# More up tiles and empty steps beside two cross attentions, and inverse norms by VectorE with products against the identity, in a one-core encoder layer

## The chip, the cores and the metric

The kernel runs on one core of one Trainium2 chip. The metric is the device time of one execution in microseconds (us); less is better. Times of several executions are given as their median with the lowest and the highest.

## What is computed

One layer of a streaming encoder is applied to 1024 prompt frames and 32 sample frames of width 1024, in float32. The parts that the change touches are the norms, the cross attention into 256 memory tokens, and the start of the MLP:

```python
def rms_norm(x, g):
    y = x * lax.rsqrt(jnp.mean(x * x, axis=-1, keepdims=True) + EPS)
    return y * g

x = x + (sigmoid(ga) * a + sigmoid(gb) * bo) @ w_mix_out      # a: window attention, bo: short convolution
hc = rms_norm(x, g_cross)
cq = hc @ w_cq                                                # 4 heads x 64
p = softmax(cq @ mem_k * MEM_SCALE)
x = x + (p @ mem_v) @ w_co
hm = rms_norm(x, g_mlp)
x = x + square(relu(hm @ w_up)) @ w_down                      # hidden 4096
```

A final RMSNorm follows; keys, values, convolution state and memory keys and values are outputs too.

## The kernel before, in words

**Layout and arithmetic.** Activations are kept transposed: 128 features on the partitions, frames along the free dimension. The 1056 frames are cut into three chunks: c=0 and c=1 with 384 frames, c=2 with 288 (256 prompt, 32 sample). A float32 operand is split into a high part (rounded to float32r) and a low part (the rest); a product is the sum of three matmuls, hi*hi, hi*lo and lo*hi (`gemm`, L183 to L185). An output tile of 128 features and one chunk is 8 blocks of 3 matmuls, 24 in all. A helper, `split` (L125, L126), makes the two parts: ScalarE copies, VectorE subtracts.

**Weights.** `item(fn, key)` appends a work item and its weights to a plan. `run` walks the plan; `issue_w` loads a weight tile of 512 KB into a ring `wr` of two buffers, and splits it into rings `wh` and `wl` of three. Weights are issued in the order of the plan, at most three ahead. Of weights that come again (`kept`), the odd ones have their low part stored in HBM the first time and loaded (L156) after that.

**The planner.** The program text gives priorities; a planner then simulates the engines' times and writes each engine's order by that simulation: if the next instruction of an engine isn't ready in the simulation, a later one that is ready goes first. On the chip every engine runs its list in order. SyncE's list holds nearly all DMA issues.

**The stretch around the change.** `trunk(c)` is eight `do_conv_out` tiles and eight `do_mix` tiles of a chunk: output of the convolution merged with the gated attention, then the mixing projection and the residual. `pump(n)` splits what was loaded at the last pump and starts n more loads of the convolution's result (L786) into temporaries; all temporaries share one ring `ct` of six buffers (NCT). `cross_steps(c)` lists the steps of a chunk's cross attention: statistics of the first norm, the query projection `do_cq`, then a pipeline over heads (`Cross.scores`, `Cross.turn`, `Cross.values`; for c=2 the sample frames are a fifth unit, and it comes first), then the two halves of the output projection `do_co`, then the statistics of the MLP's norm. `beside(steps, fillers, late)` deals them out: after each filler tile one step, so that matmuls of the fillers stand between the dependent pieces of the steps. The order is: `trunk(0)` with pumps; `trunk(2)` beside the steps of c=0; `trunk(1)` beside those of c=2; then up tiles beside those of c=1. An up tile (`do_up(j, c)`) is a `gemm` of one of the first eight weight tiles of w_up with a chunk's normed activations, a relu and a square on GpSimd (L1244), and a store.

**After the cross attention of c=1.** `normed_split(1, f)` makes the normed and split activations of chunk 1, one of eight feature blocks at a time: a product on VectorE (L1212), a store, a copy on ScalarE (L1215), a difference on VectorE (L1216). They need R[1], the inverse norm of every frame on every partition, from `chunk_stats(1)`. Then come the up tiles of chunk 1, `combine(k)` (sums and differences of normed blocks for a Strassen-like scheme; for k of 2 and 3 half of it waits in `combine_rest` until the up tiles of chunk 1 are done), and `up_start`, which begins the 12 paired tiles of that scheme with weights from `up_fetch` (L1294, L1295) and `up_issue`.

**The inverse norm.** `square_acc` squares on ScalarE (L257) and adds on GpSimd (L259). `stats_col` sums over partitions by matmuls with a vector of ones (L214), giving one value per frame with frames on the partitions, 128 x 3; then v = mean + EPS on VectorE, a square root on ScalarE (L217), a reciprocal and one Newton step on VectorE (L218 to L221). `stats_row` spreads it: for each block of 128 frames the identity is multiplied by the column on ScalarE (L229), its low part is made on VectorE (L230), and two matmuls with a 128 x 128 matrix of ones (L231, L232) put every frame's value on all partitions in PSUM; `chunk_row` copies that to R[c] (L242). `stats_col` runs 13 times and `stats_row` 12 times: for the first norm of three chunks, the memory, both later norms of three chunks, and the final norm (where chunk 1 needs no row). For chunk 1 the last `stats_col` is followed only by six scalings (L1671, L1673) and the stores of the result.

## Time and profile before

| | |
|---|---|
| time, median of 3 runs (lowest to highest) | 1803.92 us (1800.46 to 1803.97) |
| profiled execution, its own time | 1799.48 us |
| profiled execution, from first to last instruction | 1797.6 us |
| TensorE matmul busy | 1757.5 us (98%) |
| VectorE / ScalarE / GpSimd busy | 65% / 44% / 33% |
| mean granted TensorE clock | 0.991 |

The profile is of one execution. PE is TensorE's matmuls, PEld its weight loads, DVE is VectorE, ACT is ScalarE, POOL is GpSimd, SP is SyncE, which issues DMAs. Matmuls overlap: each has its start, and its end is modelled, so PE is busy without a break when the next starts before the end of the last. A row of the timeline has the start in us from the first instruction, the duration, engine, source line, operation, the tile written and those read, shapes, count, and in brackets how long the engine was idle before and what it waited for. A row of a table by stretches has the stretch, its length, each engine's busy time (and instructions), the granted clock of TensorE as a share of full speed, and the load of the DMA engines (share, GB/s).

### The profile page before, as it was taken

What the parts mean: (1) busy time and instruction counts of PE and PEld (TensorE: products, weight loads), DVE (VectorE), ACT (ScalarE), POOL (GpSimd) and SP (SyncE); (2) the same over time, 40 slices, a digit from 0 to 9 for tenths busy, and PEclk for the clock granted to TensorE, in tenths of its full rate; (3) what the DMA queues carried; (4) which work ended last, traced back from release to release, by engine and by line L of the source; (5) the groups of instructions that cost most, each with busy time, mean ns of one, the idle gap of its engine ahead of it and who ended that gap; (6) DMA issues with size and microseconds to landing.
All of it is one profiled execution on the core that took longest, in us unless ns stands there. A gap on an engine that the chain in (4) does not pass through costs nothing.

```text
span 1797.6 us, 30252 instructions
## 1 busy us (share of the span) xinstructions
PE 1757.5 (98%) x11110; PEld 1737.5 (97%) x11110; DVE 1165.8 (65%) x2165; ACT 797.8 (44%) x1566; POOL 589.3 (33%) x681
## 2 busy tenths in 40 slices
PE   8999999999999999999999899899999999999997
PEld 8999999999999999999999899799999999999997
DVE  6776767868666746556575777667556676436773
ACT  8643535435344334335575656432222343324453
POOL 0013245653453534411233232375654300100111
PEclk9999999999999999999999999899999999999999
DMA  5232234344346888767766466653433487436573
GB/s 180 102 110 92 87 106 150 117 151 145 127 151 240 302 297 287 261 211 259 252 218 224 170 211 228 223 207 133 142 126 125 158 279 247 159 125 219 187 250 119
DMA packets 183859, 331.50 MB, mean 184 GB/s; under 512 B 18768, under 2 KB 139376, under 8 KB 183584
## 3 DMA queue, kind: packets, MB, share of 16 engines
q1 hardware_dynamic: 169936, 281.18, 46.3%
q0 software_dynamic: 13776, 48.41, 7.7%
q8 instruction: 87, 1.43, 0.3%
q14 instruction: 60, 0.49, 0.1%
HBM read 242.99 MB, written 86.52 MB: 183 GB/s over the span
## 4 chain that ended last, share of the span: by engine, by line
PE 85%; DMA 7%; DVE 3%; ACT 2%; issue 1%; POOL 1%; SPq 0%; DVEq 0%; ACTq 0%; POOLq 0%
PE acc L183 13%; PE acc L185 13%; PE acc L184 13%; PE acc L1606 6%; PE acc L1605 6%; PE acc L1607 6%; PE acc L851 5%; PE acc L852 5%; PE acc L853 5%; PE pa L184 2%; PE pa L183 2%; PE pa L185 2%; PE pt L572 2%; DMA wr<-in_w_conv_out 1%; DVE wl L126 1%
## 5 line engine op out<-in xcount | busy, mean ns | idle before, releaser
L126 DVE TENSOR_TENSOR wl<-wr,wh 128x1024 fp32r<-128x1024 f32 x225 | 297.2, 1321 | 177.2 <-ACT wh L125 175.2
L125 ACT CAST wh<-wr 128x1024 fp32r<-128x1024 f32 x225 | 236.2, 1050 | 384.0 <-PE acc L1606 104.1
L183 PE MATMUL acc<-X,wh 128*128 128x384 f32 (+1 forms) x864 | 282.1, 327 | 7.9 <-ACT wh L125 7.9
L184 PE MATMUL acc<-X,wh 128*128 128x384 f32 (+1 forms) x864 | 279.4, 323 | 0.0
L185 PE MATMUL acc<-X,wl 128*128 128x384 f32 (+1 forms) x864 | 278.7, 323 | 0.3 <-DVE wl L126 0.3
L185 PE MATMUL acc<-Y,wl 128*128 128x384 f32 (+1 forms) x624 | 201.9, 325 | 1.1 <-DMA wl<-wl_d 1.1
L184 PE MATMUL acc<-Y,wh 128*128 128x384 f32 (+1 forms) x624 | 202.5, 325 | 0.0
L183 PE MATMUL acc<-Y,wh 128*128 128x384 f32 (+1 forms) x624 | 199.4, 326 | 2.8 <-ACT Y L1215 1.8
L259 POOL TENSOR_TENSOR xacc<-xacc,ct 128x384 f32<-128x384 f32 (+1 forms) x62 | 72.3, 1168 | 361.8 <-ACT ct L257 360.0
L183 PEld LDWEIGHTS acc<-X,wh 128*128 128x128 f32 x864 | 163.2, 189 | 8.6 <-ACT wh L125 7.9
L184 PEld LDWEIGHTS acc<-X,wh 128*128 128x128 f32 x864 | 163.4, 189 | 0.6
L185 PEld LDWEIGHTS acc<-X,wl 128*128 128x128 f32 x864 | 163.1, 189 | 0.8 <-DVE wl L126 0.8
L183 PEld LDWEIGHTS acc<-Y,wh 128*128 128x128 f32 x624 | 117.5, 189 | 4.2 <-ACT Y L1215 2.2
L185 PEld LDWEIGHTS acc<-Y,wl 128*128 128x128 f32 x624 | 117.9, 189 | 1.7 <-DMA wl<-wl_d 1.7
L184 PEld LDWEIGHTS acc<-Y,wh 128*128 128x128 f32 x624 | 118.0, 189 | 0.0
L1606 PE MATMUL acc<-Y,wh 128*128 128x384 f32 (+1 forms) x352 | 113.2, 322 | 0.0
L1607 PE MATMUL acc<-Y,wl 128*128 128x384 f32 (+1 forms) x352 | 112.8, 321 | 0.0
L1605 PE MATMUL acc<-Y,wh 128*128 128x384 f32 (+1 forms) x352 | 112.5, 321 | 0.0
L125 ACT CAST PTh<-pt 128x512 fp32r<-128x512 f32 (+3 forms) x94 | 46.0, 516 | 112.3 <-PE pt L572 108.4
L707 POOL TENSOR_TENSOR ws<-ws 128x256 f32<-128x256 f32 x92 | 82.3, 895 | 5.2
L1244 POOL TENSOR_TENSOR ct<-ct 128x288 f32<-128x288 f32 (+1 forms) x48 | 45.7, 955 | 116.7 <-DVE ct L1240 52.6
L853 PE MATMUL acc<-Y,wl 128*128 128x384 f32 x248 | 83.3, 336 | 0.0
(360 smaller groups left out, 4755.7 us busy)
## 6 DMA issues: line engine op xcount, KB each, us to landing
wr<-in_w_in SPq DMA_DIRECT2D x53, 512.0 KB, 3.7
wr<-in_w_up SPq DMA_DIRECT2D x48, 512.0 KB, 3.8
wr<-in_w_down SPq DMA_DIRECT2D x32, 512.0 KB, 3.9
wr<-wsum_d SPq DMA_DIRECT2D x32, 512.0 KB, 3.6
wl<-wl_d SPq DMA_DIRECT2D x28, 512.0 KB, 4.5
wr<-in_w_conv_out SPq DMA_DIRECT2D x24, 512.0 KB, 4.8
wr<-in_w_mix SPq DMA_DIRECT2D x24, 512.0 KB, 4.7
ct<-b_d SPq DMA_DIRECT2D x48, 192.0 KB, 3.9
```

Of the source, the lines that this page charges most:

```text
L125: act.copy(hi, src)
L126: dve.tensor_sub(lo, src, hi.bitcast(F32))
L183: pe.matmul(out, wh[:, a], hi, start=(k == 0), stop=False)
L184: pe.matmul(out, wh[:, a], lo, start=False, stop=False)
L185: pe.matmul(out, wl[:, a], hi, start=False, stop=(k == len(acts) - 1))
L707: pin(pool_e.tensor_tensor(t[:, to], t[:, x], t[:, y], op=ALU.add))
L851: pe.matmul(acc, wh[:, a], hi, start=(start and k == 0), stop=False, skip_group_check=True)
L852: pe.matmul(acc, wh[:, a], lo, start=False, stop=False, skip_group_check=True)
L853: pe.matmul(acc, wl[:, a], hi, start=False, stop=(k == 3), skip_group_check=True)
L1605: pe.matmul(a, wh[:, s], hi, start=(start and k == 0), stop=False, skip_group_check=True)
L1606: pe.matmul(a, wh[:, s], lo, start=False, stop=False, skip_group_check=True)
L1607: pe.matmul(a, wl[:, s], hi, start=False, stop=(stop and k == len(acts) - 1), skip_group_check=True)
```

## The change

1. **Fillers.** All eight up tiles of chunk 2 stand beside the cross attention of c=1, where five did; the other three stood after the up tiles of chunk 1.
2. **Steps.** For c=2 and c=1 the list of steps no longer begins with an empty step, so the first statistics come after the first filler and not after the second. For c=2 an empty step is put after the scores of the first unit and another before `do_co`. The steps of c=1 end after the twelfth of 16 fillers.
3. **normed_split(1)** is dealt out three after the 14th, three after the 15th and two after the 16th filler.
4. **After it** `combine(k)` follows up tile 0, 2, 4, 6 of chunk 1 (before: 1, 3, 5, 7); `up_fetch` and `up_issue` follow tiles 5 and 7 of chunk 1 (before: 6 and 7 of chunk 2); both `combine_rest` come after all up tiles of chunk 1.
5. **Pumps** in `trunk(0)`: three loads after each of the first five tiles and none after the sixth (before: two after each of the eight).
6. **Inverse norm.** The start value comes from an integer shift and a multiply-add on the bit pattern, followed by three Newton steps, all on VectorE; the square root, the reciprocal and the early call that loads its table go. The column is split into high and low parts of 128 x 3, and each is used, broadcast along the free dimension, as the stationary operand against the identity: six matmuls of 128 columns take the place of two over the whole row, and the six products with the identity on ScalarE and VectorE go.

```diff
-        v, s, y, t = (misc.tile([P, nb], F32, tag=x, bufs=2, name=nm(x)) for x in ("st_v", "st_s", "st_y", "st_t"))
+        v, y, t = (misc.tile([P, nb], F32, tag=x, bufs=2, name=nm(x)) for x in ("st_v", "st_y", "st_t"))
         dve.tensor_scalar(v, pq, 1.0 / D, EPS, op0=ALU.mult, op1=ALU.add)
-        act.activation(s, v, AF.Sqrt)
-        dve.reciprocal(y, s)
-        dve.tensor_mul(t, v, y)
-        dve.scalar_tensor_tensor(t, t, -0.5, y, op0=ALU.mult, op1=ALU.mult)
-        dve.scalar_tensor_tensor(rcol, t, 1.5, y, op0=ALU.add, op1=ALU.mult)
+        dve.tensor_single_scalar(t.bitcast(I32), v.bitcast(I32), 1, op=ALU.arith_shift_right)
+        dve.tensor_scalar(y.bitcast(I32), t.bitcast(I32), -1, 0x5F3759DF, op0=ALU.mult, op1=ALU.add)
+        for to in (y, y, rcol):
+            dve.tensor_mul(t, v, y)
+            dve.scalar_tensor_tensor(t, t, -0.5, y, op0=ALU.mult, op1=ALU.mult)
+            dve.scalar_tensor_tensor(to, t, 1.5, y, op0=ALU.add, op1=ALU.mult)
...
         pr = ps.tile([P, n], F32, tag="pt", bufs=2, name=nm("pr"))
-        dh, dl = tmp(n, F32R), tmp(n, F32R)
+        rh, rl = (misc.tile([P, len(blocks)], F32R, tag=x, bufs=2, name=nm(x)) for x in ("st_h", "st_l"))
+        dve.tensor_copy(rh, rcol)
+        dve.tensor_sub(rl, rcol, rh.bitcast(F32))
         for j, b in enumerate(blocks):
-            s, r, eye = slice(j * P, b + P), rcol[:, j : j + 1], ident[:, j * P - b :]
-            act.mul(dh[:, s], eye, r)
-            dve.scalar_tensor_tensor(dl[:, s], eye, r, dh[:, s].bitcast(F32), op0=ALU.mult, op1=ALU.subtract)
-        pe.matmul(pr, ones_r, dh, start=True, stop=False)
-        pe.matmul(pr, ones_r, dl, start=False, stop=True)
+            s, eye = slice(j * P, b + P), ident_r[:, j * P - b :]
+            for r in (rh, rl):
+                pe.matmul(pr[:, s], r[:, j : j + 1].to_broadcast([P, P]), eye, start=(r is rh), stop=(r is rl))
...
-        act.copy(ones_r, ones.to_broadcast([P, P]))
-        warm = misc.tile([P, 1], F32, name="warm")
-        act.activation(warm, ones, AF.Sqrt)
         make_identity(nc, ident)
+        act.copy(ident_r, ident)
...
-        steps = [("call", [mem_load] if c == 0 else [])]
+        steps = [("call", [mem_load])] if c == 0 else []
...
-            if c == 0 and i < nu:
+            if c == 0 and i < nu or c == 2 and i < 1:
                 steps.append(("call", []))
...
+        if c == 2:
+            steps.append(("call", []))
         steps.append(("items", [(do_co(c, 0), ("w_co", 0))]))
...
-    left = beside([], trunk(0), [(i, lambda: pump(2)) for i in range(NF)])
-    item(lambda: pump(0))
+    left = beside([], trunk(0), [(i, lambda i=i: pump(3 if i < 5 else 0)) for i in range(6)])
...
-    left = beside(left + cross_steps(1), up0(0) + up0(2)[:5])
+    left = beside(left + cross_steps(1), up0(0) + up0(2), normed(1, (13, 13, 13, 14, 14, 14, 15, 15)))
     assert not left
-    for f in range(NF):
-        item(lambda f=f: normed_split(1, f))
     for j in range(NF):
         item(*do_up(j, 1))
-        if j in (1, 3, 5, 7):
+        if j in (0, 2, 4, 6):
             item(lambda k=j // 2: combine(k))
-    for j in range(5, NF):
-        item(*do_up(j, 2))
-        if j < 7:
-            item(lambda k=j - 3: combine_rest(k))
-        if j == 6:
+        if j == 5:
             item(lambda: [up_fetch(0), up_fetch(1), up_issue(0, 1)])
         if j == 7:
             item(lambda: [up_issue(0, 2), up_issue(1, 1)])
+    item(lambda: [combine_rest(k) for k in (2, 3)])
```

More of the change, by code (lines that the diff above doesn't have):

```diff
@@ L12 @@
 F32R = mybir.dt.float32r
+I32 = mybir.dt.int32
 AF = mybir.ActivationFunctionType
@@ L68, in hybrid_step @@
     ones = misc.tile([P, 1], F32, name="ones")
-    ones_r = misc.tile([P, P], F32R, name="ones_r")
+    ident_r = misc.tile([P, P], F32R, name="ident_r")
     nsink = misc.tile([P, 20], F32, name="nsink")
```

## The prediction, made before the changed kernel was run

> **What bounds the kernel now.** I read the page first, then what TensorE waits for, then a table of stretches, then the timeline where the table shows a hole. The first lines of the page:
>
> ```profile
> span 1797.6 us, 30252 instructions
> ...
> PE 1757.5 (98%) x11110; PEld 1737.5 (97%) x11110; DVE 1165.8 (65%) x2165; ACT 797.8 (44%) x1566; POOL 589.3 (33%) x681
> ```
>
> TensorE is the bound, with 40.1 us idle in all. A reordering can only win back idle time and the slow clock that follows it; more matmul time is paid in full. The longest of TensorE's waits:
>
> ```profile
> PE acc L183 <- ACT wh L125: 9.8, 4, 7.9
> ```
>
> 7.9 us of it is the start, which waits for a weight and isn't touched. The rest lies in few places, which the stretches show:
>
> ```profile
> 820.00:860.00 40.00, 37.01 (x190) 35.71 (x189) 26.13 (x42) 19.70 (x36) 6.56 (x6) 0.91 0.72 241
> 1000.00:1040.00 40.00, 34.75 (x207) 33.25 (x206) 32.08 (x70) 26.17 (x68) 11.84 (x12) 0.91 0.44 149
> 1118.00:1160.00 42.00, 33.66 (x175) 30.85 (x176) 25.84 (x45) 19.11 (x32) 14.90 (x13) 0.88 0.63 217
> 1160.00:1187.00 27.00, 26.94 (x168) 26.70 (x167) 18.12 (x25) 12.40 (x19) 17.60 (x15) 1.00 0.95 332
> 1240.00:1280.00 40.00, 40.00 (x252) 40.00 (x252) 25.40 (x33) 9.77 (x11) 24.14 (x19) 1.00 0.40 135
> 1136.36:1146.60 10.24, 6.91 (x20) 6.39 (x21) 5.92 (x14) 3.51 (x8) 0.00 (x0) 0.50 0.44 149
> 1020.31:1023.71 3.40, 3.40 (x17) 3.38 (x17) 2.33 (x6) 1.73 (x5) 0.00 (x0) 0.50 0.01 3
> ```
>
> 1240 to 1280 is how it runs undisturbed. The three stretches on top are the seams of this change: the pumps' end, the end of the cross attention of c=2, and the passage to the up tiles of chunk 1. There the granted clock falls to half for 3.4 us or a multiple after a wait, so a hole costs its idle time and more.
>
> **The hole of chunk 1** (fillers, normed_split and combine, one edit). After the fifth up tile of chunk 2:
>
> ```profile
> 1133.67 0.83 PE L214 MATMUL pq<-ones,xacc 128*128 128x1 f32 x6 [0.80 <-POOL xacc L259]
> 1137.87 0.69 PE L231 MATMUL pr<-ct,ones_r 128*128 128x384 f32 x1 [3.37 <-ACT ct L229]
> 1140.78 1.01 PE L183 MATMUL acc<-Y,wh 128*128 128x384 f32 x2 [1.82 <-ACT Y L1215]
> ```
>
> TensorE sums, waits for the column, spreads it, waits for the first normed block. In 1118 to 1160 it is idle 42.00 - 33.66 = 8.3 us; of the 10.24 us at half clock it works 6.91, which loses 3.5. The hole costs 11.8 us. In the new order four up tiles of chunk 2 stand between the statistics and the first up tile of chunk 1. Their step:
>
> ```profile
> 1132.32 0.29 PE L183 MATMUL acc<-Y,wh 128*128 128x288 f32 x1
> 1132.44 0.29 PE L184 MATMUL acc<-Y,wh 128*128 128x288 f32 x1
> ```
>
> They start 0.12 us apart (0.125 with what rounding hides), so 24 matmuls take 3.0 us and four tiles 12. The chain from the column's sum (1133.67) to the first normed block (1140.78) took 7.1 us, so it is covered with 4.9 to spare, in which further blocks get ready. Two things remain: the 0.80 for GpSimd's squares, since one tile stands before the sum as now, and about 1.5 us of shorter waits for weights and for `do_co`'s operand. I take -9.5; ends 0 (the planner consumes the tiles earlier) and -11.8.
>
> What moves past what: the weights of three up tiles (one load of 512 KB each, a second for the odd ones) go ahead of chunk 1's on SP; the eight normed_split (on DVE twice, ACT once, SP once each) share VectorE and the six `ct` buffers with up tiles that they had nearly to themselves; the four combine (four loads each on SP, three differences on DVE, one on POOL, four splits) come one tile earlier. Nothing of this is on TensorE's path while fillers last.
>
> **The passage to `up_start`.** The three tiles of chunk 2 stood between the up tiles of chunk 1 and the first paired tiles, and covered their weights. That cover goes. SP's rows:
>
> ```profile
> 1175.96 0.33 SPq L145 DMA_DIRECT2D wr<-in_w_up  x1
> 1179.75 0.33 SPq L1294 DMA_DIRECT2D wr<-in_w_up  x1
> ```
>
> The first half of pair 0 is loaded 3.8 us behind the last up weight, less than a tile's time (4.2): the pair's weights simply continue the sequence and come as the next weight would. The DMA engines were full in 1160 to 1187 (0.95, 332 GB/s) and TensorE didn't wait; three weights fewer fall into that stretch now. `combine_rest` has the 17 us of `up_start` as its cover (48 matmuls of 384 columns at 0.175, priced below, and three tiles of 3.0). Bounds 0 and +10 (a hole like the one removed); I take +1, near the row that shows no wait.
>
> **Cross attention of c=2.**
>
> ```profile
> 1019.14 0.38 PE L1156 MATMUL o<-PTh,mv 128*128 128x256 f32 x1 [2.90 <-DVE tO L1159]
> ...
> 1025.42 0.66 PE L1183 MATMUL acc<-Y,wh 128*128 128x288 f32 x3 [1.34 <-ACT Y L1165]
> ```
>
> In 1000 to 1040 TensorE is idle 5.25 us, and the clock (0.91 of 40 us) takes 3.6 more: 8.9. Values of the last heads and the output projection run there with no filler between. The first unit begins a filler earlier and has one more behind it, and one mixing tile of 24 x 0.175 = 4.2 us now stands before `do_co`; the 1.34, the second slow stretch and the small waits should go. The 2.90 has another root:
>
> ```profile
> 1017.09 0.61 ACT L262 ACTIVATE Y<-Ga,prm 128x384 fp32r<-128x384 f32 x1 [1.33 <-DVE Ga L1045]
> ```
>
> ScalarE stood behind a residual whose load came late, and the copy that frees the buffer `o` stood behind that. The empty step moves this only by chance. I take -5; ends 0 and -8.9.
>
> **Pumps.**
>
> ```profile
> 823.20 1.01 POOL L1031 TENSOR_TENSOR ct<-ct,ct 128x384 f32<-128x384 f32 x1 [4.87 <-DMA ct<-m_d]
> 830.36 1.02 POOL L1031 TENSOR_TENSOR ct<-ct,ct 128x384 f32<-128x384 f32 x1 [6.14 <-DMA ct<-m_d]
> ...
> 833.75 0.45 PE L184 MATMUL acc<-M,wh 128*128 128x384 f32 x1 [0.69 <-DVE M L126]
> ```
>
> The merge of one tile follows the last by 7.2 us, against 4.2 of matmuls, because its second operand waits for one of six `ct` buffers, four of which the pumps hold; by the eighth tile the lag reaches the mixing tiles. 820 to 860 costs 3.0 idle and 3.6 by the clock, 6.6. Without pumps the last three tiles have the buffers to themselves; but with three loads instead of two in the first five the lag builds up earlier. Ends -6.6 and +6.6 (the same hole, earlier); I take -2, as the lag has three tiles to shrink.
>
> **The spreading of the norm.** From the chain of waits, where each piece is the time to the next, and from the groups:
>
> ```profile
> 1082.53 0.18 PE acc L183
> ...
> 1089.24 0.66 PE pt L1137 x6
> ```
> ```profile
> L231 PE MATMUL pr<-ct,ones_r x12: 279/333/688, 35.8 to 1738.7; 128*128 128x384 f32 x7, 128*128 128x288 f32 x4, 128*128 128x256 f32 x1
> ```
>
> A matmul of 384 columns steps by 0.175, one of 128 columns by 0.11: six take 0.66, two took 0.35. So +0.31 seven times, +0.40 four times (two of 288 at 0.125 went), and +0.2 for the memory (four for two): +4.0 us, in full, since these stand between fillers. Ends 0 (they fall into waits) and +8 (half clock). The Trainium skill, "TensorE: Matmul & The Clock Gate", section "Back-to-back issue gap", gives about 81 ns for a matmul of 128 columns with its weight load; by that figure the estimate would be +2.0 and the sum 2 us lower; the row here, of transposes of the same width, says 0.11.
>
> **The column on VectorE.** Six more dependent steps; on ScalarE these go, with the square root itself:
>
> ```profile
> 1134.40 1.28 ACT L217 ACT_TABLE_LOAD   x1
> ...
> 1136.83 0.98 ACT L229 ACTIVATE ct<-ident,rc 128x128 fp32r<-128x128 f32 x3 [0.88 <-DVE rc L221]
> ```
>
> ScalarE is 44% busy and such chains otherwise run beside fillers: 0, between -2.3 where a chain is waited for (1.28 + 0.98) and what the first rival below costs. At the end of the program nothing hides the steps:
>
> ```profile
> 1788.47 0.16 DVE L216 TENSOR_SCALAR st_v<-pq 128x3 f32<-128x3 f32 x1 [2.93 <-PE pq L214]
> ...
> 1789.50 0.16 DVE L221 SCALAR_TENSOR_TENSOR rc<-st_t,st_y 128x3 f32<-128x3 f32 x1
> 1789.69 2.07 DVE L1671 TENSOR_SCALAR y<-acc,rc 128x512 f32<-128x512 f32 x3
> ```
>
> From the sum to the first scaling 1.2 us; twelve steps at the pitch of 0.2 take 2.4: +1.2 (ends +0.7 and +2).
>
> **The sum.** -9.5 + 1 - 5 - 2 + 4.0 + 1.2 = -10.3 us. The profiled execution took 1799.48 (span 1797.6 and 1.9 around it), which gives 1789.2. The median of the runs shown is 4.4 above that execution, so the forecast for the median is 1803.92 - 10.3 = 1793.6, taken as 1793.5. What a measurement of this kernel can tell from no change is about 0.2%, 3.6 us.
>
> **The rivals.**
>
> *Late R blocks the accumulators (slower).* The evictions of `do_cq` need R and hold two of three accumulators until it comes:
>
> ```profile
> 974.85 0.82 DVE L1089 SCALAR_TENSOR_TENSOR ct<-acc,R 128x288 f32<-128x288 f32 x2 [1.14 <-ACT R L242]
> ```
> ```profile
> 1066.53 1.54 DVE L126 TENSOR_TENSOR wl<-wr,wh 128x1024 fp32r<-128x1024 f32 x1
> ```
>
> In the second row a weight's low part slid in between two links of the chain. If that happens before each of the six new links, a chain is 6 x (1.2 + 0.2) = 8.5 us longer, less the 2.3 that goes; with one free accumulator, some 2 us of slack (half a tile of 24 x 0.175), TensorE waits 4 us at each of three query projections, and 1.7 by the clock: +17, which gives 1810.6. It decides from 14 us in all, some 3 us of wait at each. For it: the slid-in row; against: the planner knows the links. 0.13.
>
> *The hole moves to `up_start`.* If the pair's first weight finds both `wr` buffers held, TensorE waits for load, cast and difference at the end of chunk 1: +9 on top, 1802.6. The full DMA speaks for it, the rows of SP against it. 0.17.
>
> *All seams close.* -11.8 - 8.9 - 6.6 + 5.2 = -22: 1781.8. Nothing excludes it. 0.12.
>
> *The clock isn't tied to these waits.* Only idle time would come back: 6 of the 8.3 at chunk 1, 2.6 of the 5.25 at c=2, 1 of the 3.0 at the pumps, less 5.2 and 1: -3.4, 1800.5. The Trainium skill's same page, section "What's actually happening", has the clock fall only after an idle window of about 3.4 us; by that rule these waits, none of them longer than 3.37 in the rows above, would not lower it. The trace speaks against it: half clock at 1020.31 follows 2.90 idle and is seen nowhere in 1240 to 1280. 0.06.
>
> **Numbers.** The forecast with errors of its terms, 1788 to 1799, has 0.47; 0.05 is left for what I don't see, on both sides. Range 1782 to 1804: it leaves out the late R and about half of the full closing. Faster by over 0.2% (under 1800.3): 0.47 + 0.12 + 0.03 of the clock rival + 0.06 of the moved hole + rest = 0.72; the same: 0.09; slower: 0.19.
>
> **What would show it.** Chunk 1: no wait of L231 or its successor for the column, L183 not waiting for L1215, full clock from the statistics to the up tiles; if wrong, a wait of L183 or L851 for `wh` or `wl` at `up_start`. c=2: no wait before L1183, the 2.90 perhaps still there. Pumps: L1031 at an even pace and no wait for M; if wrong, waits for L1030 while the first five tiles run. Spreading: 46 matmuls more, 0.11 apart. End: 2.4 us from L214 to L1671. The prediction is wrong if the planner's new order opens a seam that isn't there now, since every engine's list is written anew.

## The result, and the profile after

The changed kernel takes **1814.08 us** (median of 4 runs, 1811.75 to 1815.9) against 1802.19 for the kernel before (1800.43 to 1803.97). The ratio is 1.0065, with a 95% interval of 1.0046 to 1.0084. It is slower by 11.9 us where 10.3 less were forecast. The profiled execution took 1812.96 us, 13.5 more than that of before.

The page's first lines, after:

```profile
span 1811.2 us, 30363 instructions
...
PE 1761.4 (97%) x11156; PEld 1739.9 (96%) x11156; DVE 1185.2 (65%) x2245; ACT 776.2 (43%) x1509; POOL 586.9 (32%) x681
```

TensorE has the 46 matmuls more, and 3.9 us more work (1757.5 before). Its idle time grew from 40.1 to 49.8 us. So 9.7 of the 13.6 us by which the span grew are waits. In the table of what TensorE waits for, these two are the largest behind the start:

```profile
PE acc L184 <- DVE ct L1030: 8.0, 2, 6.9
PE acc L186 <- DMA wl<-wl_d: 4.3, 1, 4.3
```

Line numbers are shifted by one here: L184 to L186 are the three matmuls that were L183 to L185. In the first, 6.9 of 8.0 us are one wait; the second is a single one. The table by stretches (length, busy time of PE, PEld, DVE, ACT, POOL, then clock, DMA share and GB/s) says where the kernel loses, as the prediction's table did for before:

```profile
820.00:860.00 40.00, 32.01 (x173) 31.24 (x173) 24.93 (x42) 18.07 (x36) 6.19 (x6) 0.91 0.69 219
1000.00:1060.00 60.00, 53.96 (x316) 51.04 (x314) 46.89 (x92) 36.04 (x90) 19.73 (x18) 0.94 0.49 170
1118.00:1160.00 42.00, 39.46 (x270) 37.34 (x268) 25.52 (x49) 20.05 (x31) 16.36 (x16) 1.00 0.70 250
1160.00:1187.00 27.00, 21.63 (x105) 20.06 (x106) 15.09 (x25) 9.30 (x15) 8.09 (x8) 0.87 0.84 272
```

Idle time and half clock can't simply be added here, since half clock costs nothing while TensorE waits. What counts is the time that it works at half clock:

```profile
833.75:840.58 6.83, 3.42 (x11) 3.45 (x12) 4.90 (x9) 3.37 (x8) 1.00 (x1) 0.50 0.90 305
1175.09:1181.91 6.82, 4.52 (x14) 4.52 (x15) 3.06 (x5) 1.87 (x3) 3.16 (x3) 0.50 1.03 384
```

TensorE works 3.42 and 4.52 us of these two stretches, and half of that is lost. So the pumps cost 8.0 idle and 1.7 by the clock, 9.7, against 6.6 before. The second row is the cross attention of c=2 (60 us here, since it lies later): 6.0 idle and 3.1 by the clock, 9.1, against 8.9. In the last two rows the hole has moved. 1118 to 1160 lost 11.8 before and now 2.5 at full clock; 1160 to 1187 lost nothing before and now 5.4 idle and 2.3 by the clock, 7.6. The timeline of TensorE shows the new hole, and that of the DMA queue on SP what stands ahead of the load that it waits for:

```profile
1177.39 0.69 PE L186 MATMUL acc<-Y,wl 128*128 128x384 f32 x1 [4.27 <-DMA wl<-wl_d]
```
```profile
1160.53 1.42 SPq L1213 DMA_DIRECT2D xn_d<-ct  x2
1166.05 0.32 SPq L1263 DMA_DIRECT2D lt<-xn_d  x1
1166.47 0.38 SPq L1213 DMA_DIRECT2D xn_d<-ct  x1
...
1170.28 0.91 SPq L1263 DMA_DIRECT2D lt<-xn_d  x2
1171.24 0.48 SPq L157 DMA_DIRECT2D wl<-wl_d  x1
```

Between 1161.95 and 1166.05 SP issues nothing. Its own table of waits over 1150 to 1180 says why:

```profile
SPq L1263 <- DMA xn_d<-ct: 6.5, 2, 4.0
```

`combine` loads normed blocks that `normed_split` has just stored, so its load waits 4.0 us for the store to land. The low part that TensorE waits for is issued behind it, at 1171.24, and lands 6.1 us later. The stall is not what delays it, though. VectorE takes finished up tiles of chunk 1 out of the accumulators (L1242) at these times:

```profile
1170.58 0.56 DVE L1242 TENSOR_SCALAR ct<-acc 128x384 f32<-128x384 f32 x1 [3.27 <-PE acc L186]
...
1171.52 0.55 DVE L1242 TENSOR_SCALAR ct<-acc 128x384 f32<-128x384 f32 x1
...
1172.63 0.55 DVE L1242 TENSOR_SCALAR ct<-acc 128x384 f32<-128x384 f32 x1
```

Three tiles run interleaved, as the normed blocks arrive, and end together. The wait stands at the fourth tile (the texts put on record with the experiments call it the second). Its low part goes into the ring `wl` of three buffers, of which the first comes free when the first tile ends, at about 1170.5. The load leaves 0.7 us after that, so SP's list costs at most 0.7. In the kernel before, three tiles end together too; there SP stands idle from 1152.6 on and waits for TensorE to give the buffer back (its table of waits over 1152 to 1156):

```profile
SPq L156 <- PE acc L185: 3.3, 1, 3.3
```

That load leaves at 1155.69 and lands 3.5 us later, where the changed kernel's takes 6.1. The DMA engines are 97% busy while the latter is under way, and 73% during the former. That the loads of `combine`, bunched behind the stall, are what slows it is likely, but no run shows it.

### The profile page after: what moved, and what is told of

Same layout as the page of the kernel before. It is cut to its first block, busy times and chain, and to the rows that moved or that the text cites. A ratio compares the mean times of both kernels' runs of the same rounds, so it can differ in the third digit from the quotient of the medians.

```text
span 1811.2 us, 30363 instructions
## 1 busy us (share of the span) xinstructions
PE 1761.4 (97%) x11156; PEld 1739.9 (96%) x11156; DVE 1185.2 (65%) x2245; ACT 776.2 (43%) x1509; POOL 586.9 (32%) x681
## 5 line engine op out<-in xcount | busy, mean ns | idle before, releaser
L184 PE MATMUL acc<-X,wh 128*128 128x384 f32 (+1 forms) x864 | 282.4, 327 | 8.2 <-ACT wh L126 8.2
L185 PE MATMUL acc<-X,wh 128*128 128x384 f32 (+1 forms) x864 | 279.6, 324 | 0.0
L186 PE MATMUL acc<-X,wl 128*128 128x384 f32 (+1 forms) x864 | 278.9, 323 | 0.3 <-DVE wl L127 0.3
L184 PE MATMUL acc<-Y,wh 128*128 128x384 f32 (+1 forms) x624 | 202.1, 328 | 9.1 <-DVE ct L1030 8.0
L186 PE MATMUL acc<-Y,wl 128*128 128x384 f32 (+1 forms) x624 | 203.0, 326 | 4.3 <-DMA wl<-wl_d 4.3
L185 PE MATMUL acc<-Y,wh 128*128 128x384 f32 (+1 forms) x624 | 203.4, 327 | 0.9 <-DVE Y L1216 0.9
L184 PEld LDWEIGHTS acc<-X,wh 128*128 128x128 f32 x864 | 163.2, 189 | 8.9 <-ACT wh L126 8.2
L185 PEld LDWEIGHTS acc<-X,wh 128*128 128x128 f32 x864 | 163.6, 189 | 0.6
L186 PEld LDWEIGHTS acc<-X,wl 128*128 128x128 f32 x864 | 163.3, 189 | 0.8 <-DVE wl L127 0.8
L184 PEld LDWEIGHTS acc<-Y,wh 128*128 128x128 f32 x624 | 118.1, 190 | 11.7 <-issue 7.2
L186 PEld LDWEIGHTS acc<-Y,wl 128*128 128x128 f32 x624 | 118.4, 190 | 4.6 <-DMA wl<-wl_d 4.6
L185 PEld LDWEIGHTS acc<-Y,wh 128*128 128x128 f32 x624 | 118.6, 190 | 1.7 <-DVE Y L1216 1.7
L852 PE MATMUL acc<-Y,wh 128*128 128x384 f32 x248 | 83.8, 338 | 0.0
L851 PE MATMUL acc<-Y,wh 128*128 128x384 f32 x248 | 83.7, 338 | 0.0
```

Source lines behind the costliest of these rows:

```text
L184: pe.matmul(out, wh[:, a], hi, start=(k == 0), stop=False)
L185: pe.matmul(out, wh[:, a], lo, start=False, stop=False)
L186: pe.matmul(out, wl[:, a], hi, start=False, stop=(k == len(acts) - 1))
L851: pe.matmul(acc, wh[:, a], hi, start=(start and k == 0), stop=False, skip_group_check=True)
L852: pe.matmul(acc, wh[:, a], lo, start=False, stop=False, skip_group_check=True)
```

## The experiments

Each single edit was put on the kernel before, then parts were undone in the changed kernel, then the parts that gained were put together. Ratios are against the kernel before on the same chip, whose median was between 1802 and 1807 in these comparisons; 0.01% is 0.18 us.

| kernel | median, us | against before | interval |
|---|---|---|---|
| the whole change | 1814.08 | +0.65% | +0.46 to +0.84 |
| pumps alone | 1808.18 | +0.26% | +0.12 to +0.41 |
| norm alone | 1813.38 | +0.36% | +0.23 to +0.50 |
| steps of c=2 alone | 1812.30 | +0.30% | +0.14 to +0.45 |
| fillers alone | 1803.21 | -0.14% | -0.26 to -0.01 |
| pumps, ring of their own | 1799.75 | -0.33% | -0.48 to -0.17 |
| spreading alone | 1813.08 | +0.35% | +0.21 to +0.48 |
| column alone | 1814.11 | +0.39% | +0.23 to +0.54 |
| column, one Newton step | 1802.67 | -0.16% | -0.28 to -0.04 |
| empty steps of c=2 alone | 1801.68 | -0.27% | -0.43 to -0.12 |
| first step of c=2 dropped, alone | 1818.99 | +0.58% | +0.39 to +0.78 |
| fillers, low parts not kept | 1809.01 | +0.19% | +0.07 to +0.31 |

The four single edits sum to +0.78%, 14 us, which lies within the interval of the whole; the sum itself is uncertain by some 0.3%. The two halves of the norm do not add: +0.35% and +0.39% alone, +0.36% together. Two theories were put against each other: that every edit pays at its own place, or that the rewritten lists open holes anywhere.

### A second profile of the kernel before

No edit; it says how far two profiles of one program differ.

> The kernel before once more, for a second profile: the one shown took 1799.48 us and was the fastest of its runs. If its small losses were luck, waits that no edit touches are longer here: the wait for the gate at 684 (L962), 0 there and 1 to 2 us in the traces of the single edits, and the wait for the low weight part at the second up tile of chunk 1, 1.05 there and 2.6 to 5.2 in the others. If those waits come from the edits, both are again under 1.1.

It took 1808.0 us against 1799.48 for the profile of the prediction. TensorE's timeline, at three places:

```profile
684.88 0.41 PE L851 MATMUL acc<-X,wh 128*128 128x384 f32 x1 [1.50 <-DVE Ga L962]
...
1131.24 0.50 PE L1183 MATMUL acc<-Y,wh 128*128 128x384 f32 x1 [2.58 <-DVE ct L1240]
...
1164.58 0.44 PE L185 MATMUL acc<-Y,wl 128*128 128x384 f32 x1 [1.25 <-DMA wl<-wl_d]
```

The first wait was not there at all, the second was 0.35, the third 1.05. So the profile shown was a lucky one, and a difference of 1 to 3 us at one place between two single profiles says nothing by itself. It also says that the wait for `wl_d` stood in the kernel before already: what causes it is not new.

### The pumps

```diff
-    left = beside([], trunk(0), [(i, lambda: pump(2)) for i in range(NF)])
-    item(lambda: pump(0))
+    left = beside([], trunk(0), [(i, lambda i=i: pump(3 if i < 5 else 0)) for i in range(6)])
```

> The kernel before with the new pumps alone (three loads after each of the first five convolution tiles, none after the sixth). Theory 1 (every part pays at its own place): the wait for L1030 that the changed kernel has at 829.9 (6.89 us and half clock behind it) comes from the three loads in the ring of six temporaries, so it stands here too; 820 to 880 loses about 5 more than before, and the time is 1807. Theory 2 (the lists are written anew and the hole is an accident of the new order): no wait of 6.9 for L1030 here, and the time is within 3 us of 1802. The prediction's own term was -2: 1800.

+0.26%, and the wait stands where it stood in the whole change, with the same releaser:

```profile
825.68 0.42 PE L183 MATMUL acc<-Y,wh 128*128 128x384 f32 x1 [2.09 <-DVE ct L1030]
...
837.70 0.66 PE L183 MATMUL acc<-Y,wh 128*128 128x384 f32 x1 [7.61 <-DVE ct L1030]
```

So it is the edit's own. Whether the cause is the ring of six or SP's order, the next kernel decides: same pumps, and (once the cross attention's pool is open) a ring of three more buffers for what they load.

```diff
-wanted.extend((bcp[c], k, bc_d[c][:, k], CH[c][1], lambda c=c: yslot(c)) for k in range(NF))
+wanted.extend((bcp[c], k, bc_d[c][:, k], lambda c=c: cr.tile([P, CH[c][1]], F32, tag="pm", bufs=3, name=nm("pm")) if cr else tmp(CH[c][1]), lambda c=c: yslot(c)) for k in range(NF))
```

> The new pumps alone, but the loads of the pumps go into a ring of three buffers of their own instead of the shared ring of six. Theory 1 (three loads in the ring of six take the buffers that the evictions and the merge's operand need): the wait for L1030 at 829 (7.6 us with the new pumps) is under 1.5, the hole with its half clock is gone, and the time is 0.4% below that of the new pumps with the shared ring, at or below before. Theory 2 (the hole comes from SP's order: the merge's operand is loaded behind two weights and three pump loads, 6 us to landing): the wait stays at 4 or more, and the time is within 0.1% of the new pumps alone.

From +0.26% to -0.33%: the ring. The stretch 820 to 880 of the two kernels, shared ring first:

```profile
820.00:880.00 60.00, 50.30 (x282) 49.72 (x281) 35.38 (x55) 28.75 (x51) 12.12 (x11) 0.94 0.74 237
```
```profile
820.00:880.00 60.00, 57.06 (x343) 55.94 (x342) 42.37 (x62) 31.84 (x53) 14.22 (x12) 1.00 0.81 269
```

9.7 us idle become 2.9, and the clock stays up. The merges on GpSimd follow each other at 4.0 and 4.3 us, and the last two at 6.0 and 5.5, where the prediction quoted 7.2 for before:

```profile
814.04 1.10 POOL L1031 TENSOR_TENSOR ct<-ct,ct 128x384 f32<-128x384 f32 x1 [2.52 <-DMA wr<-in_w_conv_out]
818.06 1.94 POOL L1031 TENSOR_TENSOR ct<-ct,ct 128x384 f32<-128x384 f32 x1 [2.92 <-DVE ct L1030]
822.40 1.00 POOL L1031 TENSOR_TENSOR ct<-ct,ct 128x384 f32<-128x384 f32 x1 [2.40 <-DMA ct<-m_d]
828.38 1.87 POOL L1031 TENSOR_TENSOR ct<-ct,ct 128x384 f32<-128x384 f32 x1 [4.98 <-DVE ct L1030]
833.84 1.25 POOL L1031 TENSOR_TENSOR ct<-ct,ct 128x384 f32<-128x384 f32 x1 [3.59 <-ACT Y L781]
```

What the three buffers would do for the old pumps was not run, so the gain against before isn't split between the pumps and the buffers.

The same edit of the ring in the changed kernel, all else as it is:

> The changed kernel with one thing changed: the loads of the pumps have a ring of three of their own. Alone, the ring took the new pumps from +0.26% to -0.33%. Theory 1 (parts add): the changed kernel's +0.65% becomes +0.05%, and its wait of 6.9 us for L1030 at 830 is under 1.5. Theory 2 (in company the hole only moves, to the mixing tiles or the first cross attention): +0.4% or more.

1806.85 us, +0.15% (0.05 to 0.26) against before, so 0.50% below the changed kernel, near the 0.59 that the ring was worth alone. The wait for L1030 is gone there too; the one for `wl_d` is 6.8 us there, in place of 4.3.

### The steps of c=2

```diff
-        steps = [("call", [mem_load] if c == 0 else [])]
+        steps = [("call", [mem_load] if c == 0 else [])] if c != 2 else []
...
-            if c == 0 and i < nu:
+            if c == 0 and i < nu or c == 2 and i < 1:
...
+        if c == 2:
+            steps.append(("call", []))
```

> The kernel before with the new steps of c=2 alone (no empty first step, one empty step after the first unit's scores, one before the output projection; the steps of c=1 as before). Theory 1: the empty steps do not carry the values past the last fillers, since the planner starts do_co while values are still running; the wait of about 1.3 for the operand of do_co and one for a value (L1156) stay, and the time is 1802 to 1805. Theory 2: the empty steps do their work and what spoils them in the changed kernel is the norm's longer column: 1797 (the term of -5).

+0.30%, more than either theory gave, with a wait of 2.6 us for L1089 at 979. So the three edits were taken apart. First the two empty steps alone (the last two hunks):

> The kernel before with the two empty steps of c=2 alone; its empty first step stays, so the statistics come after the second filler as before. The three edits to the steps of c=2 together cost 0.30%. Theory 1 (the statistics one filler earlier are what costs: the inverse norm comes late, 2.6 us of wait for L1089 at 979): without that, within 0.1% of before, or faster by the term of -5 (0.28%). Theory 2 (the empty steps themselves cost: VectorE has its own work of each further filler ahead of the links of the heads, and the output projection still waits 1.3 us for its operand): 0.2% or more slower, with 12 us or more lost in 1000 to 1060 against 11.

-0.27%: faster by 4.9 us, the term of -5. Then only the first hunk:

> The kernel before with only the empty first step of c=2 dropped. Theory 1: 0.15% to 0.3% slower, with a wait for L1089 at the query projection of c=2. Theory 2: within 0.1% of before; every later step one filler earlier leaves one more filler behind the output projection.

+0.58%, 10.5 us slower. The two add up to the +0.30% of all three. The stretch 1000 to 1060 of the kernel before, of the empty steps alone, and of the dropped step alone (columns as above):

```profile
1000.00:1060.00 60.00, 54.75 (x325) 53.25 (x324) 47.53 (x95) 37.70 (x86) 21.05 (x21) 0.94 0.50 168
```
```profile
1000.00:1060.00 60.00, 56.88 (x349) 55.84 (x349) 48.27 (x95) 37.43 (x83) 25.08 (x21) 0.97 0.54 177
```
```profile
1000.00:1060.00 60.00, 52.79 (x309) 50.21 (x308) 43.67 (x95) 38.06 (x95) 14.70 (x16) 0.91 0.48 165
```

Idle time and work at half clock cost 8.7, 4.8 and 11.6 (9.3 in the second profile of before). So this stretch holds most of the gain, but only 2 to 3 of the 10.5 us that the dropped step costs. With the empty steps the wait of 2.90 for `o` (L1159) is gone as well. With the step dropped the query projection waits for the inverse norm:

```profile
981.29 0.44 PE L183 MATMUL acc<-Y,wh 128*128 128x384 f32 x1 [1.92 <-DVE ct L1089]
```

The empty first step had kept the last statistics of c=0 and the first of c=2 two fillers apart. With that wait and the stretch less than half of the 10.5 is found; the rest is not located. Then the step was given back to the changed kernel, all else as it is:

```diff
-        steps = [("call", [mem_load])] if c == 0 else []
+        steps = [("call", [mem_load] if c == 0 else [])] if c != 1 else []
```

> The changed kernel with one edit undone: the steps of c=2 begin with the empty step again. The changed kernel stands at +0.65% against before. Theory 1 (the dropped step costs about 0.58% wherever it stands, by two statistics next to each other and every head beside earlier fillers): between +0.05% and +0.2%. Theory 2 (its price is the late inverse norm at the query projection, a wait that the changed kernel does not have): still +0.5% or more.

1816.41 us, +0.54% (0.39 to 0.69). That is a gain of 0.11%, less than the intervals allow to tell from nothing, and not the 0.58 that the step costs alone. The changed kernel has no wait for L1089 around 980, so part of what the step costs alone isn't there to be won. What takes the rest stays open: parts of the steps do not add in that company.

### The norm

```diff
-        act.activation(s, v, AF.Sqrt)
-        dve.reciprocal(y, s)
...
+        dve.tensor_single_scalar(t.bitcast(I32), v.bitcast(I32), 1, op=ALU.arith_shift_right)
...
+        for to in (y, y, rcol):
...
+                pe.matmul(pr[:, s], r[:, j : j + 1].to_broadcast([P, P]), eye, start=(r is rh), stop=(r is rl))
```

> The kernel before with the new inverse norm alone (column on VectorE, spreading by products with the identity). Theory 1: 46 more matmuls at 0.11 less what two longer ones took, +3.9, and about +1.2 at the end of the program: 1807.3; the hole of chunk 1 stays near the 11.8 us that it has in the kernel before. Theory 2: the longer column makes values late elsewhere too (waits of L1183, L1187 or L1216 that were not there before), and the time is 1812 or more. Below 1804 if the chain is really shorter by the table load and the products on ScalarE.

+0.36%, 6.5 us; the sum for it was 5.2. Then its halves, the spreading alone (`stats_row`) and the column alone (`stats_col`):

> The kernel before with only the spreading changed (six products with the identity for two over the row; column with the square root as before). The whole norm alone cost 0.36% (6.5 us). Theory 1 (the price is TensorE's products): +3.9, so 0.22%, and no new wait. Theory 2 (the price is the column's longer chain): less than +2, within 0.1% of before.

> The kernel before with only the column changed (shift, multiply-add and three Newton steps on VectorE; spreading with the row of ones as before, no square root). Theory 1: +1.2 at the end of the program and nothing mid kernel: 0.07%. Theory 2 (twelve dependent steps late on a busy VectorE): +3 or more, 0.17% and over, with longer waits for the column at the statistics of chunk 1 (3.4 us before). A gain of about 2 if the table load and the square root were what the waits were made of.

+0.35% and +0.39%. The spreading's interval (3.8 to 8.7 us) reaches down to the 3.9 us of its products, but its profile also has a wait that neither profile of before has, in 1000 to 1060:

```profile
1000.00:1060.00 60.00, 51.29 (x296) 49.17 (x296) 46.90 (x96) 38.97 (x93) 18.37 (x18) 0.89 0.51 171
```
```profile
PE pt L1137 <- DVE PTl L126: 4.2, 1, 4.2
```

The stretch loses 14.5 us here, 8.7 and 9.3 in the profiles of before. The whole norm has the same products and waits 1.2 us at L1137, so the products do not bring that wait wherever they stand. The column's price is no end effect of 1.2 us, so its length was cut:

```diff
-        for to in (y, y, rcol):
+        for to in (rcol,):
```

> The kernel before with the new column, but one Newton step where the change has three (six of twelve links less; the inverse norms are then not exact). The full column alone cost 0.39%. Theory 1 (the price is the chain's length on VectorE): half of it or less, +0.1% to +0.2%, and the way from the column's sum to the spreading at c=2 falls from 8.3 and 8.7 us to about 6.5. Theory 2 (the price comes from elsewhere, such as ScalarE's lists without the square root): +0.3% or more.

-0.16%: six links fewer are worth 0.55%, and with a short column VectorE's way is better than the square root. The way from the column's sum to the spreading at c=2 falls from 8.0 and 9.2 us to 6.9 and 6.7. TensorE's timeline at two statistics with three Newton steps (the first norm of c=2, and the last of chunk 1), and then with one step (the last of chunk 1):

```profile
976.76 0.40 PE L233 MATMUL pr<-ct,ones_r 128*128 128x288 f32 x1 [0.64 <-ACT ct L231]
...
1148.21 0.69 PE L233 MATMUL pr<-ct,ones_r 128*128 128x384 f32 x1 [4.51 <-ACT ct L231]
```
```profile
1142.14 0.69 PE L233 MATMUL pr<-ct,ones_r 128*128 128x384 f32 x1 [3.62 <-ACT ct L231]
```

The wait of 4.51 and then 3.62 was 3.37 in the kernel before. The timeline of VectorE in the kernel with three steps shows how links get late:

```profile
1052.85 0.16 DVE L222 SCALAR_TENSOR_TENSOR st_t<-st_t,st_y 128x3 f32<-128x3 f32 x1
1053.39 1.23 DVE L127 TENSOR_TENSOR wl<-wr,wh 128x1024 fp32r<-128x1024 f32 x1 [0.38 <-ACT wh L126]
1054.54 0.16 DVE L223 SCALAR_TENSOR_TENSOR st_y<-st_t,st_y 128x3 f32<-128x3 f32 x1
```

Two links of 0.16 us that could follow at 0.2 lie 1.7 apart, because the difference of a weight, and the wait for its cast, slid in between. The waits shown here are 1.8 us of the 7 (0.64, and 4.51 less 3.37); where the rest goes isn't shown. That a shorter chain comes sooner and the time falls is shown. How much of the 0.55% is the chain itself is not: every list is written anew here too, and the halves of the norm do not add.

Last, the whole change with the old norm:

> The changed kernel with the old inverse norm. Theory 1 (parts add): 0.65 less 0.36, +0.3%. Theory 2 (with the fillers beside it the longer column is covered, and only the products and the end of the program cost, 5.1 us): +0.37%. Below +0.2% if the norm costs more in company, since its longer column is added where two statistics stand next to each other.

+0.44% (0.29 to 0.59): in company the norm costs 0.21%, 3.8 us, with an interval that reaches from nothing to beyond the 6.5 of the norm alone. This kernel does show the wait for L1089 (2.35 us at 980), which the changed kernel lacks.

### The fillers

```diff
-    left = beside(left + cross_steps(1), up0(0) + up0(2)[:5])
+    left = beside(left + cross_steps(1), up0(0) + up0(2), normed(1, (13, 13, 13, 14, 14, 14, 15, 15)))
...
-        if j in (1, 3, 5, 7):
+        if j in (0, 2, 4, 6):
             item(lambda k=j // 2: combine(k))
```

> The kernel before with the fillers of c=1 alone (all eight up tiles of chunk 2, normed_split and combine moved, no empty first step of c=1; old norm, old pumps, old steps of c=2). Theory 1: the hole of 11.8 us goes, and a wait for a low weight part loaded back from HBM (wl<-wl_d, 4.3 us with 3.4 by the clock in the changed kernel) takes its place at the second up tile of chunk 1, since the issue of that load stands on SP behind the loads of combine: -2 to -4, 1799. Theory 2: that wait is an accident of the new order, and alone the edit brings the term of -9.5: 1793.

-0.14%, 2.5 us; the terms for it came to -8.5. The statistics are waited for no more, and the wait for the low part is most of what is left (the profiled execution took 1809.16 us, 6 more than the median). So the low part was no longer taken from HBM, but made each time by VectorE:

```diff
-    for name, n in (("w_conv_out", NF), ("w_mix", NF), ("w_cq", 2), ("w_co", 2), ("w_up", NF)):
+    for name, n in (("w_conv_out", NF), ("w_mix", NF), ("w_cq", 2), ("w_co", 2)):
```

> The fillers of c=1 alone, and the odd weights of w_up no longer keep their low part in HBM: VectorE makes it each time (eight more differences of 1.2 us). Theory 1 (what is left at chunk 1 is the load of a low part, issued on SP behind loads that wait for the stores of the normed blocks): the 5.2 us wait with its half clock goes, and the time is 6 to 8 us below the fillers alone, 0.5% below before. Theory 2 (the up tiles of chunk 1 wait for whatever comes next: the high part, or the normed blocks): a wait of 3 or more stays at the first three up tiles of chunk 1, and the time is within 0.15% of the fillers alone.

+0.19%: 0.33% worse than the fillers alone. The hole is in TensorE's timeline of both, fillers alone first:

```profile
1171.44 0.69 PE L185 MATMUL acc<-Y,wl 128*128 128x384 f32 x1 [5.20 <-DMA wl<-wl_d]
```
```profile
1198.49 0.69 PE L851 MATMUL acc<-Y,wh 128*128 128x384 f32 x1 [5.85 <-ACT s L1347]
```

Both theories fall. The wait at the fourth tile goes: VectorE makes the low part there with 0.30 us of waiting, so what was missing is the time of the load. A longer wait stands 27 us later, behind the first paired tiles, where the kernel before has three tiles of chunk 2 as cover. TensorE comes to the first of them at 1186.82, and with the low parts kept at 1193.73, without a wait. The time that the edit took from there is missed as soon as TensorE arrives sooner.

### Together

Fillers, and pumps with their ring:

> The two parts that gained, together: the fillers of c=1, and the new pumps with a ring of three of their own; old norm, old steps of c=2. If the parts add, 0.33 and 0.14: 0.47% below before, 1797.6 on a chip where before is 1806. If the order of all lists decides more than the parts, anywhere between 0 and 0.33% below.

1799.25 us, -0.48% (-0.64 to -0.31). With the two empty steps of c=2 as well (its first step kept, the old norm):

> Everything that gained alone, together: the fillers of c=1, the new pumps with a ring of their own, and the two empty steps of c=2 with its empty first step kept; old norm. If the parts add: 0.48 and 0.27, so 0.75% below before, and no wait above 1.5 us between 820 and 1060. If the empty steps only gain because they move the end of c=2 against the up tiles: no better than 0.5% below.

**1794.25 us** (1790.56 to 1797.84) against 1805.31, ratio 0.9931, interval 0.9913 to 0.995. It beats both kernels. The parts add up nearly (0.75 expected). TensorE has no wait at the pumps at all; `wl_d` is what remains:

```profile
PE acc L185 <- DMA wl<-wl_d: 5.7, 4, 4.5
```

For that, two tiles of chunk 2 were set behind the first two up tiles of chunk 1:

```diff
-up0(0) + up0(2), normed(1, (13, 13, 13, 14, 14, 14, 15, 15))
+up0(0) + up0(2)[:6], normed(1, (11, 11, 11, 12, 12, 12, 13, 13))
...
         item(*do_up(j, 1))
+        if j < 2:
+            item(*do_up(6 + j, 2))
```

> The best kernel so far (fillers, ring, empty steps; 0.69% below before), with two of the eight up tiles of chunk 2 moved behind the first and the second up tile of chunk 1; three still stand between the statistics and chunk 1. Theory 1 (what is missing there is time, about 5 us until the low part has landed): each tile brings 3 us, the wait of 4.5 us for it falls under 1.5, its half clock (3.4) goes, and the time is 3 to 6 us lower, 0.9% below before. Theory 2 (the load is ordered behind the stores and loads of the normed blocks, however long the tiles ahead of it are): the same wait within 1 us, and the time within 0.15% of the best so far.

In this kernel the first three normed blocks are dealt out ahead of the statistics, so they are scaled with the inverse norm of the query projection and needn't wait for the right one; that flatters its time. It took 1795.22 us, -0.51% (-0.68 to -0.34), no better than the last. The wait for `wl_d` is under 1 us, as the theory of time has it, but the gain isn't there: TensorE waits at the normed blocks (1.66) and at the first paired tiles (1.76):

```profile
1136.85 0.44 PE L183 MATMUL acc<-Y,wh 128*128 128x384 f32 x1 [1.66 <-ACT Y L1215]
...
1174.24 0.56 PE L851 MATMUL acc<-Y,wh 128*128 128x384 f32 x1 [1.76 <-ACT wh L125]
```

## Why the prediction was wrong

Against the single edits the terms are off by 10.4 us for the steps of c=2, 6.7 for the pumps, 6.0 for the fillers and 1.3 for the norm, all towards slower. Three steps failed: the dropped first step was priced at nothing, the pumps' price was taken from the wrong end, and the moved work was taken to be off TensorE's path.

**The fillers, -9.5 and +1: the step that failed is "nothing of this is on TensorE's path while fillers last".** The statistics and the first normed block are covered, as said, by three tiles of 3.2 us (the prediction says four of 3.0; its two rows happen to lie 0.12 apart where their neighbours lie 0.13 apart). The path was followed only as far as the first tile of chunk 1. What became the limit is the fourth tile: its low part can be loaded only when the first of three interleaved tiles gives its buffer back, and the load then takes 6.1 us in place of 3.5. The place was in the profile of before, as one wait of 1.05 for `wl_d`. The rival "the hole moves" had the price nearly right (9 said, 7.6 lost) and a mechanism of the kind, a load that finds its buffers held, but was given another ring and the wrong place: the fourth up tile first, and `up_start` once that is mended (5.85 us idle). Measured: -2.5 in place of -8.5.

**The steps of c=2, -5: the gain was right, and the cost was not seen at all.** The two empty steps alone gave -4.9. The dropped first step, told in the list of the change, got no term; alone it costs 10.5. Part of its mechanism stood among the rivals ("late R blocks the accumulators"), but was put on the longer column, not on statistics that come a filler sooner beside the last ones of c=0. In the changed kernel itself that wait doesn't appear, and undoing the step there gains little; why the price alone and in company differ stays open.

**The pumps, -2 between -6.6 and +6.6: the value was taken from the wrong end.** +4.7. The mechanism of the upper end ("the same hole, earlier") is what the runs show, with the ring as its cause. The argument for -2 was that three tiles are left for the lag to shrink. That is not how it goes: the eviction itself (L1030) needs a buffer of the ring, and TensorE waits for the eviction, so the lag is paid at once.

**The column, 0 mid kernel: mis-sized when it stands alone.** Alone it costs 7 us, with half the links it gains 2.9. The bound from below (-2.3, what goes) was near for a short column, and the rival's slid-in row is what happens to a long one. Together with the spreading the term was near: 5.2 said for both, 6.5 measured (4.2 to 9.0), so part of the column's 7 belongs to its own lists. The end was priced right. VectorE from the column to the first scaling, after:

```profile
1801.39 0.16 DVE L217 TENSOR_SCALAR st_v<-pq 128x3 f32<-128x3 f32 x1 [2.92 <-PE pq L215]
...
1803.56 0.16 DVE L223 SCALAR_TENSOR_TENSOR rc<-st_t,st_y 128x3 f32<-128x3 f32 x1
1803.75 2.07 DVE L1667 TENSOR_SCALAR y<-acc,rc 128x512 f32<-128x512 f32 x3
```

2.36 us where 2.4 was said, at 0.2 a link.

**The spreading, +4.0: right for the products.** They follow each other at 0.11:

```profile
1152.33 0.27 PE L234 MATMUL pr<-ident_r,st_l 128*128 128x128 f32 x1
1152.44 0.27 PE L234 MATMUL pr<-ident_r,st_h 128*128 128x128 f32 x1
1152.55 0.28 PE L234 MATMUL pr<-ident_r,st_l 128*128 128x128 f32 x1
```

TensorE's busy time grew by 3.9 at the same mean clock (0.991). The run of the spreading alone cost 6.3, with the wait at L1137 on top. The Trainium skill, "TensorE: Matmul & The Clock Gate", section "Back-to-back issue gap", would have made the estimate half of that with its 81 ns; the trace has 0.11 us.

**The clock is tied to the waits**, as the forecast had it: half clock for 6.8 us in each of the holes at 834 and 1175. Not every wait brings it: the second profile of before is idle for 5.5 us in 820 to 880 at full clock. The rival that the clock isn't tied to them (1800.5) gave a gain, and the time went the other way.

**The frame.** The sum was made against a profile that was 4.4 us under its median, and the small waits that it lacked were taken as absent. And each term was taken as a gain at one hole, with the next hole priced at 1.

## What to carry to other kernels

Cover that is moved is not made: tiles put ahead of one wait are missing at the next, so follow the edit past its hole, along every queue and every ring of buffers, to the place where the moved work stood. When a load comes late, ask first when its buffer came free: here a queue that stood still for 4.0 us ahead of it looked like the cause and could explain 0.7. And an edit of several hunks should be priced hunk by hunk: here one of them (a line that only drops an empty step) cost alone twice what another gained. A dependent chain on a busy engine costs by what slides in between its links, and so by their number. Prices taken alone need not add: the halves of the norm did not.

## What the runs showed of the hardware

Half clock needs no long wait. In the kernel with the empty steps of c=2, TensorE ran at half clock for 3.41 us while busy all the time, after waits of 0.76, 1.43 and 0.22 us in the four us before and none longer:

```profile
1029.41:1032.82 3.41, 3.41 (x15) 3.41 (x14) 2.46 (x6) 2.57 (x6) 1.21 (x2) 0.50 0.18 63
```

The Trainium skill's page on TensorE named above, section "What's actually happening", has the clock fall after an idle window of about 3.4 us; read as one wait of that length, this run disagrees. Nor does the length of a single wait decide: in the second profile of the kernel before a wait of 2.87 us at 849 left the clock at 1.00 in the whole stretch, where the prediction's row of 2.90 is followed by half clock:

```profile
849.17 0.44 PE L183 MATMUL acc<-M,wh 128*128 128x384 f32 x1 [2.87 <-ACT wh L125]
```
```profile
820.00:880.00 60.00, 54.49 (x319) 52.60 (x318) 36.33 (x56) 30.50 (x52) 11.68 (x11) 1.00 0.74 244
```

And one program differs between executions at places that no edit touches: the wait at 684 was 0 in one profile and 1.50 in another.
